# Hybrid SSD and linear-attention layer: output gates projected in the gate stages, scan steps at half pieces, first block from columns

## The chip, the cores and the metric

The kernel runs on one core of a Trainium2 chip, as one program. The metric is the device time of the whole program in microseconds (us). Engines are named as in the profile: PE (TensorE, the matrix engine), DVE (VectorE), ACT (ScalarE), POOL (GpSimd), SP (SyncE, which here issues most DMAs).

## The reference

One decoder layer over 16 meta tokens and 2048 real tokens of width 1024, in float32:

```
u = rmsnorm(h, norm_w);  proj = u @ w_in  -> z, xbc, dt, q, k, v, g_gla, a_lr, merge_g
xbc = silu(conv4(xbc))                       # Mamba-2 SSD branch, 16 heads in 4 groups
y_ssd = rmsnorm((ssd_scan(xbc, dt) + d_skip * xs) * silu(z)) * ssd_norm_w
log_a = log_sigmoid(a_lr @ gate_w2 + b) / 16 # gated linear attention (GLA), 4 heads
o = gla_scan(q / sqrt(128), k, v, log_a)     # S_t = diag(a_t) S_{t-1} + k_t^T v_t; o_t = q_t S_t
y_gla = rmsnorm(o) * gla_norm_w * silu(g_gla)
merged = sum over branches of sigmoid(merge_g) * (y_branch @ w_branch)
out = rmsnorm(h + merged @ w_out)[16:] * final_norm_w
```

`g_gla`, 1024 columns of `w_in` (256 a head), is the GLA branch's output gate. It is used only in `silu(g_gla)`.

## The kernel before

All float32 products are made of three matmuls in a split form: each operand is written as a high and a low part (`split`, `load_w`), and `accum` issues high x high, high x low and low x high (L186, L187, L188).

The **first part** walks through four blocks of 512 tokens (the first with the 16 meta tokens beside them). A block has eight pieces: four SSD groups (`ssd_proj`, pieces 0 to 3), then four GLA heads (`gla_proj`, pieces 4 to 7). A piece is a generator that issues projections of the normalised input `u` (PSUM tiles `pj`) and yields between them; at each yield `step()` advances by one step everything in the list `running`: the scan of the piece before (`ssd_scan`, `gla_scan`), the making of the gates, the fetching of the next block's `u` (`fetch_u`, which runs `load_u`), and sums for the second part (`beside_unit`). PE and SP work through their instructions in exactly the order in which this code issues them (`manual_schedule`); the order of the other engines is laid out by the scheduler.

A projected tile of 128 features (`proj_feat`) is 24 matmuls of 512 columns, in two halves of 12, each with its weights of 512 KB (`whl`), loaded by SP from a split copy in memory (`k_s`, `k_g`, `k_v`, `k_z`). In block 0 the weights come raw (`wr`), are split by ACT and POOL (L173, L174), and are stored for the other blocks. An SSD group has four features (numbers 0 to 15 over the groups, `k_s0` to `k_s15`); each goes through a convolution, of which ACT does the first steps (L466, L467) into a tile `acc`. A GLA head has q, k (one feature each), v (`proj_tok`, four quarters of 24 matmuls of 256 columns) and the two gate features (`gs`, L622 to L627): PE projects, ACT takes tanh (L625), and DVE makes (tanh + 1) times the gate (L626), so that `gla_scan` can multiply its result by it at its end (L796).

`gla_scan` begins when its head's projections are all issued, and so runs beside the next head's. It advances through levels of 64 down to 2 (`level_in`, `level_out`), then sums over features (L754), transposes (L769), and goes over four chunks: products into `pc`, one with the state `s_gla` (L780), then the state's update on DVE (L781), which reads `pc` and which the next chunk's L780 needs.

`load_u` for a block after the first reads the rows of x in four steps, each in two halves (L255 loads into a tile `acc`, L256 squares with a running sum on ACT), then the columns in eight steps (loaded into `acc`, scaled on DVE at L289, rounded to the high part by ACT at L291, stored, and the low part made on DVE at L293). `acc` has two buffers; the SSD convolution uses the same two.

The **second part** is seven stages (for each half of the tokens a gate stage and two branch stages; then the output), each a large product in the seven-product form: units of pairs of 2 x 2 blocks with the products in the order `PS`, 12 matmuls of 512 columns each (PSUM tiles `psa`, `psb`, `psc`), `use` for every finished quarter, `fetch` for what `use` needs, and sums of operands (`make_sums`) prepared beforehand. The gate stage makes tanh of `merge_g` in 8 such pairs. `at(position, action)` places loads and sums by position in the list of products.

Of the kernel before, what the change touches and what calls it, by code (L numbers as in the profile page):

```python
# [36 lines left out]
T_GATE = 32  # L37


@with_exitstack  # L40
def trunk_kernel(ctx: ExitStack, tc: tile.TileContext, xm, xmt, w_feat, w_tok, w_zm, w_br, w_o,
# [22 lines left out]
    y_left = [[[left(f"y{n}_{b}_{kt}") for kt in range(KT)] for b in range(nblk)] for n in range(2)]  # L64

# [35 lines left out]
    def braw_y(n, s):  # L101
        return lambda k, t: y_left[n][2 * s + t][k]
# [10 lines left out]
    for s in range(nsb):  # L113
        b = 2 * s + 2
        if b < nblk:
            beside.update({(b, 0): ("b", 0, s), (b, 4): ("b", 1, s)})
        else:
            late += [("b", 0, s), ("b", 1, s)]
        if 0 < s:
            beside[b - 1, 0] = ("g", s)  # L120
# [43 lines left out]
    def load_w(key, src):  # L164
        n = src.shape[-1]
        hl = mk(wpool, [P, 2, 512], F32R, "whl", bufs=4)[:, :, :n]
        if key in kept:
            nc.sync.dma_start(hl.bitcast(F32), kept[key])
        else:
            save(2)  # L170
            raw = mk(wpool, [P, 512], F32, "wr", bufs=NWR)[:, :n]
            nc.sync.dma_start(raw, src)
            nc.scalar.activation(hl[:, 0], raw, AF.Copy)  # L173
            nc.gpsimd.tensor_tensor(hl[:, 1], raw, hl[:, 0].bitcast(F32), op=ALU.subtract)  # L174
            kept[key] = wdram.tile([P, 2, n], F32, tag="k_" + key, name="k_" + key, bufs=1)
            unsaved.append((kept[key], hl.bitcast(F32)))
# [13 lines left out]
    def proj_feat(key, src, segs, moving):  # L190

        pss = [bank(pj, "pj") for _ in segs]
        for half in range(2):
            h, lo = load_w(f"{key}_{half}", src[:, half * 512:(half + 1) * 512])
# [7 lines left out]
    def proj_tok(key, src, u, starts, banks, width=256, per=2, sub=None):  # L202
# [5 lines left out]
        for q0 in range(0, nq, 2):  # L208
            if q0 == nq // 2:
                yield  # L210
            ws = [load_w(f"{key}_{q}", src[:, q * per * width:(q + 1) * per * width]) for q in (q0, q0 + 1)]
            for i, ((bk, ps), a) in enumerate(zip(banks, starts)):
                c0 = sub if sub is not None and i >= NCH else 0
# [23 lines left out]

    def load_u(b):
        m0 = META if b == 0 else 0
        row0 = META - m0 + b * BLK  # L240
        tt = m0 + BLK
        pair = mk(upool, [P, 2, KT * (META + BLK)], F32R, "u")[:, :, :KT * tt]
        uh, ul = [pair[:, i].rearrange("p (k t) -> p k t", k=KT) for i in range(2)]

        def rows_rstd(r0, n):
            ss = mk(sm, [P, 1], F32, "ss")
            if m0:
                xt = mk(wk, [P, D], F32, "tok4", bufs=NT4)
                nc.sync.dma_start(xt[:n], xm[r0:r0 + n, :])
                nc.scalar.activation(xt[:n], xt[:n], AF.Square, accum_out=ss[:n])  # L250
            else:
                s2 = mk(sm, [P, 2], F32, "ss2")
                for i in range(2):
                    xt = mk(wk, [P, META + BLK], F32, "acc")[:, :BLK]
                    nc.sync.dma_start(xt, xm[r0:r0 + n, i * BLK:(i + 1) * BLK])  # L255
                    nc.scalar.activation(xt, xt, AF.Square, accum_out=s2[:, i:i + 1])  # L256
                nc.vector.tensor_tensor(ss, s2[:, 0:1], s2[:, 1:2], op=ALU.add)
# [6 lines left out]
        for c in range(NCH):  # L264
            rs.append(rows_rstd(META + b * BLK + c * P, P))
            yield
        if m0:
            rs.append(rows_rstd(0, META))
            nc.sync.dma_start(cst[:, :2], cf32[:, :2])
            nc.sync.dma_start(pv, pvec)  # L270
# [3 lines left out]
        rbs = [(rb, m0, BLK)]  # L274
        if m0:
            rm = bank(pt, "pt")
            nc.tensor.matmul(rm[:, :META], rs[NCH][:META].to_broadcast([META, P]), ident[:META, :META],
                             start=True, stop=True)
            rbs = [(rm, 0, META)] + rbs
        else:  # L280
            rbc = mk(wk, [P, 3 + META + BLK], F32, "cin")[:, :BLK]
            nc.scalar.activation(rbc, rb, AF.Copy)
            rbs = [(rbc, 0, BLK)]
            yield
        for kt in range(KT):
            xk = mk(wk, [P, META + BLK], F32, "acc")[:, :tt]
            nc.sync.dma_start(xk, xmt[:, kt, row0:row0 + tt])
            for ps, a, n in rbs:
                nc.vector.scalar_tensor_tensor(xk[:, a:a + n], xk[:, a:a + n], norm_w[:, kt:kt + 1], ps[:, :n],  # L289
                                               op0=ALU.mult, op1=ALU.mult)  # L290
            nc.scalar.activation(uh[:, kt, :tt], xk, AF.Copy)  # L291
            nc.scalar.dma_start(u_left[b][kt], xk[:, m0:])
            nc.vector.tensor_tensor(ul[:, kt, :tt], xk, uh[:, kt, :tt].bitcast(F32), op=ALU.subtract)  # L293
# [8 lines left out]
    for _ in fetch_u(0):  # L302
        pass

# [17 lines left out]
    w2r = mk(wk, [P, META + BLK], F32, "act", bufs=NACT)[:48, :512]  # L322
# [119 lines left out]
    def ssd_proj(o, g):  # L442
# [16 lines left out]
        for j in range(4):  # L459
            ti = g * 4 + j  # L460
            pss = proj_feat(f"s{ti}", w_feat[T_SSD + ti], o.segs_all, o.mov)
# [24 lines left out]
    def ssd_scan(o, g, feats, zs):  # L486
# [88 lines left out]
        if m0:  # L575
            meta_state()
        for c in range(1, NCH):
# [9 lines left out]
        for j in range(2):  # L587
# [3 lines left out]
            yo = mk(wk, [P, BLK], F32, "gg", bufs=4)  # L591
# [4 lines left out]
    def gla_proj(o, h):  # L596
# [7 lines left out]
        for ps, (a, n) in zip(proj_feat(f"g{t0 + 1}", w_feat[t0 + 1], o.segs_all, o.mov), o.segs_all):  # L604
            nc.scalar.activation(kf[:, a:a + n], ps[:, :n], AF.Copy)
        yield
# [8 lines left out]
        yield from proj_tok(f"v{h}", w_tok[SG + h], o.u, o.starts + [0] * o.ci0, places)  # L615
# [4 lines left out]
        yield  # L620
        gs = []
        for j in range(2):  # L622
            ps, = proj_feat(f"g{t0 + 2 + j}", w_feat[t0 + 2 + j], o.segs_real, o.mov)
            gg = mk(wk, [P, BLK], F32, "gg", bufs=4)
            nc.scalar.activation(gg, ps, AF.Tanh, scale=0.5)  # L625
            nc.vector.scalar_tensor_tensor(gg, gg, 1.0, ps, op0=ALU.add, op1=ALU.mult)  # L626
            gs.append(gg)  # L627
            yield
        begin(gla_scan(o, h, qs, kf, (vh, vl), vm, gs))

    def gla_scan(o, h, qs, kf, vt, vm, gs):
# [160 lines left out]
        for j in range(2):  # L792
# [3 lines left out]
            nc.vector.scalar_tensor_tensor(gs[j], ps, hgw[:, j:j + 1], gs[j], op0=ALU.mult, op1=ALU.mult)  # L796
        yield
        for j in range(2):
            nc.scalar.dma_start(y_left[1][o.b][2 * h + j], gs[j])
# [4 lines left out]
    def begin(gen):  # L804
        begun.append(gen)

    def step():
# [12 lines left out]
    with tc.manual_schedule(engines={mybir.EngineType.PE, mybir.EngineType.SP}):  # L820
        for b in range(nblk):
            o = new_block(b, next_u[b])
            for i in range(SG + GH):
# [4 lines left out]
                if i == SG and b + 1 < nblk:  # L828
                    begin(fetch_u(b + 1))
                for _ in ssd_proj(o, i) if i < SG else gla_proj(o, i - SG):  # L830
                    step()
# [116 lines left out]
    def gate_stage(s):  # L948
        def use(n, i, t, ps, snap):
# [5 lines left out]
        return Stage(f"gate{s}", ("g", s), 8,  # L955
                     lambda n, i, j: w_feat[T_GATE + 2 * n + i, :, j * BLK:(j + 1) * BLK].rearrange(
                         "p (k c) -> p k c", c=P), use)
# [202 lines left out]
```

## Time and profile before

| | |
|---|---|
| median of 3 runs | 2352.43 us (2346.6 to 2354.13) |
| profiled execution | 2356.86 us, its span 2355.0 us |
| PE busy | 2255.4 us (96%) |
| DVE, ACT, POOL busy | 1562.0 (66%), 1189.1 (50%), 684.2 us (29%) |
| mean granted clock of PE | 0.98 |
| DMA | 518.06 MB, mean 220 GB/s |

Busy time is the union of an engine's instructions, so that PE at 96% of the span has about 100 us without any matmul. The chain that ended last is the work followed back from the last instruction, and a wait is named by the instruction whose end released it.

### The profile page before, as it was taken

The numbers are of one execution on the slowest core, as the hardware profiler recorded it, in microseconds if no ns is written. First come the engines' busy times: TensorE is split into PE (matmuls) and PEld (weight loads), VectorE is DVE, ScalarE is ACT, GpSimd is POOL, SyncE is SP. The second block draws the span as 40 slices with busy tenths as digits, with TensorE's granted clock in tenths as the row PEclk, the third lists the DMA queues.
The fourth block names the chain that finished last, engine by engine and source line by source line (L and its number), as shares of the span: only waits on it lengthen the run. The fifth ranks groups of instructions, "written<-read, shape, count | busy, mean of one in ns | idle before, by whom it ended". The sixth has DMA issues, their size and how long they took to land.

```text
span 2355.0 us, 36504 instructions
## 1 busy us (share of the span) xinstructions
PE 2255.4 (96%) x12641; PEld 1968.2 (84%) x12641; DVE 1562.0 (66%) x2889; ACT 1189.1 (50%) x2764; POOL 684.2 (29%) x681
## 2 busy tenths in 40 slices
PE   6899999999999999999999999889999999999998
PEld 6889889888888988888988898768788788777886
DVE  4676665676675667566558555664679854788876
ACT  4665655465544455543455443454554454544543
POOL 3343433122321212221122200207424254322441
PEclk8999999999999999999999999989999999999999
DMA  8665875666786666787666655456668866778752
GB/s 274 212 215 183 296 255 192 202 220 218 248 282 191 207 224 208 254 268 221 193 217 216 206 167 163 136 181 226 218 222 275 277 215 213 253 244 274 236 192 108
DMA packets 301546, 518.06 MB, mean 220 GB/s; under 512 B 27696, under 2 KB 143664, under 8 KB 301360
## 3 DMA queue, kind: packets, MB, share of 16 engines
q1 hardware_dynamic: 200112, 402.32, 52.7%
q10 hardware_dynamic: 101248, 113.41, 13.8%
q8 instruction: 99, 1.62, 0.3%
q14 instruction: 87, 0.71, 0.1%
HBM read 368.42 MB, written 147.19 MB: 219 GB/s over the span
## 4 chain that ended last, share of the span: by engine, by line
PE 66%; DMA 12%; DVE 10%; ACT 5%; issue 4%; POOL 2%; SPq 1%; ACTq 0%; DVEq 0%; POOLq 0%
PE pj L186 11%; PE pj L188 11%; PE pj L187 11%; PE psa L186 4%; PE psa L187 4%; PE psa L188 4%; PE psb L187 2%; PE psb L188 2%; PE psb L186 2%; DMA acc<-in_xmt 2%; PE pc L556 2%; DMA br<-br_t 2%; PE pc L690 1%; DVE b L894 1%; PE pc L780 1%
## 5 line engine op out<-in xcount | busy, mean ns | idle before, releaser
L186 PE MATMUL pj<-u,whl 128*128 128x512 f32 (+1 forms) x1184 | 447.4, 378 | 8.3 <-ACT g_all L429 3.3
L188 PE MATMUL pj<-u,whl 128*128 128x512 f32 (+1 forms) x1184 | 431.6, 365 | 0.8 <-POOL whl L174 0.8
L187 PE MATMUL pj<-u,whl 128*128 128x512 f32 (+1 forms) x1184 | 430.7, 364 | 0.0
L186 PE MATMUL pj<-whl,u 128*128 128x256 f32 (+1 forms) x992 | 291.5, 294 | 8.1 <-ACT u L291 5.5
L188 PE MATMUL pj<-whl,u 128*128 128x256 f32 (+1 forms) x992 | 285.2, 287 | 0.7 <-DVE u L293 0.7
L187 PE MATMUL pj<-whl,u 128*128 128x256 f32 (+1 forms) x992 | 285.1, 287 | 0.6 <-POOL whl L174 0.5
L186 PE MATMUL psa<-b,a 128*128 128x512 f32 x640 | 253.5, 396 | 19.0 <-ACT sn L934 17.0
L186 PEld LDWEIGHTS pj<-u,whl 128*128 128x128 f32 x1184 | 225.7, 191 | 46.2 <-ACT g_all L429 3.7
L188 PEld LDWEIGHTS pj<-u,whl 128*128 128x128 f32 x1184 | 225.2, 190 | 36.8 <-POOL whl L174 1.1
L187 PEld LDWEIGHTS pj<-u,whl 128*128 128x128 f32 x1184 | 225.7, 191 | 33.3
L187 PE MATMUL psa<-b,a 128*128 128x512 f32 x640 | 252.8, 395 | 0.0
L188 PE MATMUL psa<-b,a 128*128 128x512 f32 x640 | 252.5, 395 | 0.0
L918 DVE TENSOR_TENSOR a<-ar,a 128x512 fp32r<-128x512 f32 x160 | 151.1, 950 | 82.1 <-ACT a L917 81.9
L186 PEld LDWEIGHTS pj<-whl,u 128*128 128x128 f32 x992 | 192.3, 194 | 9.2 <-ACT u L291 6.0
L187 PEld LDWEIGHTS pj<-whl,u 128*128 128x128 f32 x992 | 192.4, 194 | 1.7 <-POOL whl L174 1.3
L188 PEld LDWEIGHTS pj<-whl,u 128*128 128x128 f32 x992 | 192.4, 194 | 1.5 <-DVE u L293 1.5
L80 POOL TENSOR_TENSOR wr<-wr 128x256 f32<-128x256 f32 x80 | 67.0, 838 | 432.0 <-DMA wr<-y 172.1
L174 POOL TENSOR_TENSOR whl<-wr,whl 128x512 fp32r<-128x512 f32 (+1 forms) x100 | 133.5, 1342 | 188.9 <-ACT whl L173 141.3
L908 POOL TENSOR_TENSOR as<-ar,ar 128x512 f32<-128x512 f32 x40 | 59.3, 1482 | 422.4 <-DMA ar<-in_w_feat 124.3
L894 DVE TENSOR_TENSOR b<-br,b 128x512 fp32r<-128x512 f32 x196 | 149.2, 784 | 45.3 <-ACT b L893 44.8
L471 DVE SCALAR_TENSOR_TENSOR acc<-cin,hcw,acc 128x512 f32<-128x512 f32 (+1 forms) x192 | 156.6, 816 | 24.7 <-ACT acc L467 24.1
L893 ACT ACTIVATE b<-br 128x512 fp32r<-128x512 f32 x196 | 119.1, 626 | 93.5 <-DMA br<-br_t 34.7
(267 smaller groups left out, 5077.9 us busy)
## 6 DMA issues: line engine op xcount, KB each, us to landing
whl<-k_s SPq DMA_DIRECT2D x96, 512.0 KB, 4.4
whl<-k_g SPq DMA_DIRECT2D x96, 512.0 KB, 4.1
whl<-k_v SPq DMA_DIRECT2D x48, 512.0 KB, 3.8
whl<-k_z SPq DMA_DIRECT2D x36, 512.0 KB, 3.8
wr<-in_w_feat SPq DMA_DIRECT2D x64, 256.0 KB, 4.5
k_s<-whl SPq DMA_DIRECT2D x32, 512.0 KB, 3.6
cb<-cumd ACTq DMA_DIRECT2D x64, 256.0 KB, 5.6
y<-gg ACTq DMA_DIRECT2D x64, 256.0 KB, 4.5
```

The source lines that it names most:

```text
L80: nc.gpsimd.tensor_tensor(o, x, y, op=ALU.subtract)
L174: nc.gpsimd.tensor_tensor(hl[:, 1], raw, hl[:, 0].bitcast(F32), op=ALU.subtract)
L186: nc.tensor.matmul(ps, sh, mh, start=first, stop=False, **kw)
L187: nc.tensor.matmul(ps, sh, ml, start=False, stop=False, **kw)
L188: nc.tensor.matmul(ps, sl, mh, start=False, stop=last, **kw)
L471: nc.vector.scalar_tensor_tensor(acc, cin[:, k:k + tt], hcw[:, ti, k:k + 1], acc, op0=ALU.mult, op1=ALU.add)
L556: nc.tensor.matmul(py[:, h * 64:(h + 1) * 64], dm[:, h], xdt[:, h], start=True, stop=True)
L690: nc.tensor.matmul(ps[:, r * P:(r + 1) * P], kq[:, 2 * r * P:(2 * r + 1) * P], kq[:, (2 * r + 1) * P:(2 * r + 2) * P], start=True, stop=True)
L893: nc.scalar.activation(t[:, 0], raw, AF.Copy)
L894: nc.vector.tensor_tensor(t[:, 1], raw, t[:, 0].bitcast(F32), op=ALU.subtract)
L908: nc.gpsimd.tensor_tensor(s1, a21, a22, op=ALU.add)
L918: nc.vector.tensor_tensor(t[:, 1], src, t[:, 0].bitcast(F32), op=ALU.subtract)
```

## The change

1. **The output gates move.** `gla_proj` no longer projects the gate features, and `gla_scan` no longer multiplies by them: its last step scales on ACT (`yo`) and stores. Each gate stage has four more pairs (12 in place of 8), the first eight alternating between the GLA heads' gates and merge gates. For a head's pair, `fetch` reads the stored `y`, and `use` multiplies it by the projected gate and by (tanh + 1) and stores the result (`yg_left`), which branch 1 then reads.
2. **Half steps.** `gla_proj` yields after every half piece with `HALF`; `step` counts fractions and advances a generator when its count reaches one. `gla_scan` is begun before the last half of its head, with a rate of 1.5. SSD groups still step by whole pieces.
3. **The next block's input** is begun with SSD group 3 (`i == SG - 1`), where it was begun with GLA head 0.
4. **The first block** takes its mean squares from the columns alone (`first_u`): eight column loads on two queues, squares on ACT, sums on DVE, and a product with ones; the stores of this `u` go to SP between the weight loads.
5. All sums of the GLA branch's results (`("b", 1, s)`) become late ones with new positions.

Core of the diff:

```diff
@@ gla_proj
-        ps, = proj_feat(f"g{t0}", w_feat[t0], o.segs_real, o.mov)
+        ps, = yield from proj_feat(f"g{t0}", w_feat[t0], o.segs_real, o.mov, HALF)
         nc.scalar.activation(qs[:, :BLK], ps, AF.Copy, scale=QSCALE)
-        yield
+        yield HALF
...
-        yield
-        gs = []
-        for j in range(2):
-            ps, = proj_feat(f"g{t0 + 2 + j}", w_feat[t0 + 2 + j], o.segs_real, o.mov)
-            gg = mk(wk, [P, BLK], F32, "gg", bufs=4)
-            nc.scalar.activation(gg, ps, AF.Tanh, scale=0.5)
-            nc.vector.scalar_tensor_tensor(gg, gg, 1.0, ps, op0=ALU.add, op1=ALU.mult)
-            gs.append(gg)
-            yield
-        begin(gla_scan(o, h, qs, kf, (vh, vl), vm, gs))
+        begin(gla_scan(o, h, qs, kf, (vh, vl), vm), 1.5)
+        yield HALF
@@ gla_scan, last steps
-            nc.vector.scalar_tensor_tensor(gs[j], ps, hgw[:, j:j + 1], gs[j], op0=ALU.mult, op1=ALU.mult)
-        yield
-        for j in range(2):
-            nc.scalar.dma_start(y_left[1][o.b][2 * h + j], gs[j])
+            yo = mk(wk, [P, BLK], F32, "gg", bufs=3)
+            nc.scalar.activation(yo, ps, AF.Identity, scale=hgw[:, j:j + 1])
+            nc.scalar.dma_start(y_left[1][o.b][2 * h + j], yo)
@@ step
-        for gen in list(running):
-            if next(gen, running) is running:
-                running.remove(gen)
+        for e in list(running):
+            e[2] = e[2] + part * e[1] if part else 1.0
+            if e[2] >= 1:
+                e[2] -= 1
+                if next(e[0], running) is running:
+                    running.remove(e)
@@ walk over blocks and pieces
-                if i == SG and b + 1 < nblk:
+                if i == SG - 1 and b + 1 < nblk:
                     begin(fetch_u(b + 1))
@@ first_u
+        for kt in range(KT):
+            xs.append(mk(wk, [P, META + BLK], F32, "act", bufs=NACT))
+            (nc.scalar if kt % 2 else nc.sync).dma_start(xs[kt], xmt[:, kt, :tt])
...
+        for kt in range(KT):
+            nc.scalar.activation(sq[kt // 2][:, kt % 2], xs[kt], AF.Square)
+            if kt:
+                nc.vector.tensor_tensor(total, total, sq[kt // 2][:, kt % 2], op=ALU.add)
@@ gate_stage, use
+            if head(n) is not None:
+                y = got.pop((n, i, t))
+                nc.vector.tensor_tensor(y, y, x, op=ALU.mult)
             th = io() if snap is None else snap
             nc.scalar.activation(th, x, AF.Tanh, scale=0.5)
-            store(g_left[2 * s + t][2 * n + i], th)
+            if head(n) is not None:
+                nc.vector.scalar_tensor_tensor(y, th, 1.0, y, op0=ALU.add, op1=ALU.mult)
+                store(yg_left[2 * s + t][2 * head(n) + i], y)
+            else:
+                store(g_left[2 * s + t][2 * gate(n) + i], th)
```

How this moves instructions is seen in the order of single engines. First SP in block 1, before: the weight loads of SSD features 13 to 15 and, after the dots, of the second GLA feature of head 0 (`k_g17`); `whl` is a weight tile, `acc ... <-in_xm` one half of the next block's rows.

```order
L168 DMA whl_1143_7060<-k_s13_0_2570 128x1024
L168 DMA whl_1144_7074<-k_s13_1_2601 128x1024
L76 DMA wr_1148_7100<-in_w_o 128x256 x2
L76 DMA wr_1149_7101<-in_w_o 128x256 x2
L168 DMA whl_1161_7144<-k_s14_0_2685 128x1024
L168 DMA whl_1162_7158<-k_s14_1_2716 128x1024
L168 DMA whl_1176_7224<-k_s15_0_2798 128x1024
L168 DMA whl_1177_7238<-k_s15_1_2829 128x1024
...
L255 DMA acc_1196_7332<-in_xm 128x512
L255 DMA acc_1197_7335<-in_xm 128x512
L168 DMA whl_1201_7344<-k_g17_0_2957 128x1024
L168 DMA whl_1202_7358<-k_g17_1_2988 128x1024
```

The rows were read among the GLA features, two loads ahead of `k_g17`. Now the same queue in the same block, from feature 12 on:

```order
L171 DMA whl_1090_6697<-k_s12_0_2481 128x1024
L171 DMA whl_1091_6711<-k_s12_1_2512 128x1024
L309 DMA acc_1107_6778<-in_xm 128x512
L309 DMA acc_1108_6781<-in_xm 128x512
L171 DMA whl_1111_6789<-k_s13_0_2590 128x1024
L171 DMA whl_1112_6803<-k_s13_1_2621 128x1024
L78 DMA wr_1116_6829<-in_w_o 128x256 x2
L78 DMA wr_1117_6830<-in_w_o 128x256 x2
L309 DMA acc_1130_6874<-in_xm 128x512
L309 DMA acc_1131_6877<-in_xm 128x512
L171 DMA whl_1134_6885<-k_s14_0_2717 128x1024
L171 DMA whl_1135_6899<-k_s14_1_2748 128x1024
```

A pair of row loads now stands ahead of the weights of feature 13, and another ahead of those of feature 14.

ACT before, around the squares of those rows (`pj_1160` and `pj_1175` are the products of features 14 and 15):

```order
L466 ACTIVATE cin_1163_7172<-pj_1160_7143 128x512
L467 ACTIVATE acc_1164_7173<-pj_1160_7143,hcb_359,hcw_357 128x512
...
L466 ACTIVATE cin_1178_7252<-pj_1175_7223 128x512
L467 ACTIVATE acc_1179_7253<-pj_1175_7223,hcb_359,hcw_357 128x512
L256 ACTIVATE acc_1196_7332,ss2_1195_7331<-acc_1196_7332 128x512
L256 ACTIVATE acc_1197_7335,ss2_1195_7331<-acc_1197_7335 128x512
```

And now (`pj_1089` is the product of feature 12, `acc_1107` and `acc_1108` are the two halves of the rows):

```order
L501 ACTIVATE cin_1092_6725<-pj_1089_6696 128x512
L502 ACTIVATE acc_1093_6726<-pj_1089_6696,hcb_371,hcw_369 128x512
L581 ACTIVATE sq_1143_6940<-sq_1143_6940 128x512
L519 DMA cb_1196_7237<-cumd_772_4918 128x4x128
L576 ACTIVATE bt_1099_6750<-pt_1096_6741 128x128
L310 ACTIVATE acc_1107_6778,ss2_1106_6777<-acc_1107_6778 128x512
L310 ACTIVATE acc_1108_6781,ss2_1106_6777<-acc_1108_6781 128x512
L606 ACTIVATE junk_1104_6774,ssq_1077_6663<-tok4_1076_6662 128x256
L509 ACTIVATE act_1094_6734<-acc_1093_6726 128x512
```

The squares of a pair of row halves stood behind the convolution of feature 15, the last of the group; now they stand behind that of feature 12, and those of the next pair (not shown) behind that of feature 13.

PE in `gla_scan` of a head in block 1, before: from a sum over features (`pt_1434`) to the product with the state. The dots ahead of the second transposing pair and ahead of `pc` each stand for the rest of 24 matmuls of one gate feature, those behind the first `pc` for its other five.

```order
L754 MATMUL pt_1434_8661<-sq_1426_8612,ones_r_245 128x512
L186 MATMUL pj_1438_8672<-u_420_2935,whl_1439_8673 128x512
...
L769 MATMUL pt_1442_8706<-cst_243,sq_1435_8665 128x128 x2
L186 MATMUL pj_1444_8712<-u_420_2935,whl_1445_8713 128x512
...
L186 MATMUL pc_1451_8750<-tok4_1318_7945,kdt_1392_8395 128x256
...
L780 MATMUL pc_1451_8750<-s_gla_250,act_1379_8319 128x256
```

And now, in a head of the same block; here the dots stand for the rest of 24 matmuls of a part of v:

```order
L783 MATMUL pt_1362_8115<-sq_1352_8044,ones_r_277 128x512
L191 MATMUL pj_1356_8050<-whl_1366_8126,u_312_2338 128x256
...
L798 MATMUL pt_1368_8154<-cst_275,sq_1363_8119 128x128 x2
L191 MATMUL pj_1357_8051<-whl_1366_8126,u_312_2338 128x256
...
L191 MATMUL pc_1371_8191<-tok4_1275_7622,kdt_1320_7906 128x256
...
L809 MATMUL pc_1371_8191<-s_gla_282,act_1307_7832 128x256
```

The steps of the scan stood 24 matmuls of 512 columns apart, and now stand 24 of 256 columns apart.

More of the change, by code (lines that the diff above doesn't have):

```diff
@@ L300, in fetch_u @@
         next_u[b] = yield from load_u(b)
[L302 to L303 removed]
+    next_u[0] = first_u()
     nc.sync.dma_start(cst[:, 2:], cf32[:, 2:])
@@ L614, in gla_proj @@
             places.append((2, pv5[:, :256]))
-        yield from proj_tok(f"v{h}", w_tok[SG + h], o.u, o.starts + [0] * o.ci0, places)
+        yield from proj_tok(f"v{h}", w_tok[SG + h], o.u, o.starts + [0] * o.ci0, places, part=HALF)
         if m0:
```

167 lines of the change are left out of this document (104 added, 63 removed).

## The prediction

> **What bounds the kernel now.** I read the page first, then the waits of PE by stretch, then the timelines of the two places that the change moves.
>
> ```profile
> span 2355.0 us, 36504 instructions
> PE 2255.4 (96%) x12641; PEld 1968.2 (84%) x12641; DVE 1562.0 (66%) x2889; ACT 1189.1 (50%) x2764; POOL 684.2 (29%) x681
> PE 66%; DMA 12%; DVE 10%; ACT 5%; issue 4%; POOL 2%; SPq 1%; ACTq 0%; DVEq 0%; POOLq 0%
> ```
>
> PE is busy for 96% of the span, and no other engine for more than 66% (DVE). So a matmul taken away is time gained, as long as everything that PE needs still comes in time; the chain's 12% on DMA and 10% on DVE say where it might not. The waits of PE in block 1 from its last SSD group on, then those of the stretch from 765 to 1475 us, and last those of the second part, with the total, the count and the longest in us:
>
> ```profile
> PE pc L780 <- DVE s_gla L781: 3.0, 1, 3.0
> PE pc L556 <- DVE sq L547: 1.7, 1, 1.7
> PE pj L186 <- DMA whl<-k_g: 0.9, 1, 0.9
> ...
> PE pc L780 <- DVE s_gla L781: 4.8, 3, 2.5
> PE pc L556 <- DVE sq L547: 1.8, 1, 1.8
> PE pj L186 <- DMA whl<-k_g: 0.6, 1, 0.6
> ...
> PE psa L186 <- ACT sn L934: 17.0, 6, 4.3
> ```
>
> In blocks 1 to 3 PE loses very little: the rows that the trace lists are ten waits in 900 us, the longest 3.0 us. The order of work has been fitted so that weights, rows and scan steps arrive just in time, and the change takes cover from two of these fits.
>
> **Matmuls that go.** Consecutive starts on PE give the price of one matmul; the last two rows are from the table of windows (length, then busy time of PE, PEld, DVE, ACT, POOL, the granted clock, DMA share, GB/s):
>
> ```profile
> 693.75 0.39 PE L186 MATMUL pj<-u,whl 128*128 128x512 f32 x1
> 693.97 0.39 PE L187 MATMUL pj<-u,whl 128*128 128x512 f32 x1
> ...
> 707.65 0.28 PE L187 MATMUL pc<-tok,kdt 128*128 128x256 f32 x1
> 707.77 0.28 PE L188 MATMUL pc<-tok,kdt 128*128 128x256 f32 x1
> ...
> 707.00:765.00 58.00, 55.00 (x323) 48.59 (x322) 33.44 (x76) 23.71 (x70) 8.07 (x9) 0.97 0.60 191
> ...
> 1590.00:1649.00 59.00, 59.00 (x262) 48.87 (x261) 28.57 (x32) 26.07 (x46) 43.65 (x41) 1.00 0.68 224
> ```
>
> A 512-wide one takes 0.22 to 0.23 us (262 of them fill the 59.00 us of the last row: 0.225), a 256-wide one 0.12. The change removes the two gate projections of each GLA head from the first part: 16 heads x 2 x 24 = 768 matmuls. It adds four pairs to each of the two gate stages, at seven products of 12 matmuls: 2 x 4 x 84 = 672. All are 512 wide, all on a full PE: 96 x 0.227 = 21.8 us less. By the Trainium skill (page "TensorE: Matmul & The Clock Gate", section "Back-to-back issue gap") a warm 512-wide matmul follows the last after 512/2.4 + 2.5 = 216 ns, which would make it 20.7; the trace here shows a little more, and I keep the trace's. The gate's ACT and DVE work moves with it; the gate stage has room for it, with DVE busy 28.57 and ACT 26.07 of 59 us.
>
> **The row loads go into the last SSD group.** This is the largest term. The next block's rows are now read during SSD group 3 and no longer during GLA head 0. What such a load does to the queue behind it can be seen at its present place. Rows of SP (issuing), ACT and PE of block 1:
>
> ```profile
> 588.49 9.63 SPq L168 DMA_DIRECT2D whl<-k_s  x4
> 611.22 5.82 SPq L255 DMA_DIRECT2D acc<-in_xm  x2
> 617.15 0.85 SPq L168 DMA_DIRECT2D whl<-k_g  x2
> ...
> 592.24 0.63 ACT L546 ACTIVATE sq<-sq 128x512 f32<-128x512 f32 x1 [2.61 <-POOL wr L80]
> 606.89 0.28 ACT L541 ACTIVATE bt<-pt 128x128 f32<-128x128 f32 x1 [0.22 <-DVE tok L538]
> 614.81 0.60 ACT L466 ACTIVATE cin<-pj 128x512 f32<-128x512 f32 x1 [1.04 <-PE pc L559]
> 615.30 0.78 ACT L467 ACTIVATE acc<-pj,hcb,hcw 128x512 f32<-128x512 f32 x1
> 615.96 0.63 ACT L256 ACTIVATE acc<-acc 128x512 f32<-128x512 f32 x1
> ...
> 612.75 1.00 PE L556 MATMUL pc<-c,sq 128*128 128x64 f32 x8
> 614.07 0.59 PE L559 MATMUL pc<-c,bt 128*128 128x256 f32 x2
> 621.01 0.50 PE L186 MATMUL pj<-u,whl 128*128 128x512 f32 x1 [0.86 <-DMA whl<-k_g]
> ```
>
> The two halves of a row load go through `acc`, which has two buffers and is also the SSD convolution's. The second half waits on SP until ACT has squared the first (L256), that square stands in ACT's order behind the convolution's start (L466, L467), and the weight loads stand behind both on SP. So from L466 (614.81) it is 2.3 us to the issue of the `k_g` loads (617.15) and 6.2 us to the matmul that needs them (621.01). It costs 0.86 us only because, between that feature's matmuls and the waiting ones, PE has a scan step (612.75 to about 614.5) and another feature, q, of 24 x 0.227 = 5.4 us, whose weights were already there.
>
> In the new place the same chain stands between one SSD feature and the next, twice in a group: the loads for features 13 and 14 are issued behind a row's second half, and that waits for ACT behind L501 and L502 of the feature just before. The cover is then the scan step alone, 2.1 us. The chain: 0.2 us from the last matmul to ACT, the 6.2 us above, and the two ACT rows that now stand in between (0.63 and 0.28, shortened by their overlap to 0.8) make 7.2; less 2.1 of cover it is 5.1 us, four times in blocks 1 and 2: +20.4. Before, the four `k_s` loads of 588.49 were issued a piece ahead and cost PE nothing. The ends: 3 us each where ACT takes the square early, 6.5 where the loads land slower. For the second there is a reason, since DMA is full in that group already (1.03 below), and 2 MB of rows come into it.
>
> ```profile
> 589.00:597.00 8.00, 8.00 (x43) 6.79 (x42) 5.60 (x12) 4.38 (x11) 4.57 (x6) 1.00 1.03 323
> ...
> whl<-k_s SPq DMA_DIRECT2D x96, 512.0 KB, 4.4
> wr<-in_w_feat SPq DMA_DIRECT2D x64, 256.0 KB, 4.5
> ...
> L174 POOL TENSOR_TENSOR whl<-wr,whl 128x512 fp32r<-128x512 f32 (+1 forms) x100 | 133.5, 1342 | 188.9 <-ACT whl L173 141.3
> ```
>
> A weight load of 512 KB takes 4.4 us to land. By the Trainium skill (page "DMA: Bandwidth & Descriptors", section "Anatomy of one DMA — SWDGE (gpsimd) path": about 2.0 us and then bytes at 436 GB/s) it would be 3.2 us, an estimate for a single transfer on another issue path, and each stall would be 1.2 us shorter. With some 200 to 320 GB/s already moving the row is what counts.
>
> In block 0 the features' weights come raw (4.5 us) and go through a split on ACT and POOL (1.3 us for POOL's part), with the store of the last ones queued between. That is longer by 1 to 2 us than in the other blocks, but the split of the loads into halves lets part of it run ahead: 3 to 8 us each; I take 5, twice: +10. The column loads that now precede the k weights cost 0 to 4 us in each of three blocks: +6, less the waits that go with the old place, 0.9 and 0.6 above and about 2.5 in block 0: +2. While PE stands still, ACT and DVE catch up, and the two waits on L547 (1.7 and 1.8) go: -3.5.
>
> **Steps at half pieces.** Between the scan's products of the last level (L754, now L783) and its state update (L781, now L810) PE used to do 48 matmuls of 512. Now it does 48 of 256, the v pieces: 48 x (0.227 - 0.12) = 5.1 us less cover. How near the limit this was, in block 1:
>
> ```profile
> 695.79 0.63 PE L754 MATMUL pt<-sq,ones_r 128*128 128x512 f32 x2
> 712.50 1.22 PE L780 MATMUL pc<-s_gla,act 128*128 128x256 f32 x2 [2.96 <-DVE s_gla L781]
> ...
> 698.69 0.68 DVE L626 SCALAR_TENSOR_TENSOR gg<-gg,pj 128x512 f32<-128x512 f32 x1
> 699.28 0.44 DVE L756 COPY_PREDICATED c<-msk,pt 128x256 f32<-128x256 uint8 x1
> 704.92 1.22 DVE L289 SCALAR_TENSOR_TENSOR acc<-acc,pv,cin 128x512 f32<-128x512 f32 x1
> 708.34 0.68 DVE L293 TENSOR_TENSOR u<-acc,u 128x512 fp32r<-128x512 f32 x1
> 711.97 0.47 DVE L781 SCALAR_TENSOR_TENSOR s_gla<-s_gla,egl,pc 128x256 f32<-128x256 f32 x1
> ```
>
> PE came from the last L754 (ends about 696.2) to the L780 that needs the update after 13.3 us, at 709.5, and then stood 2.96 us. It now comes after 13.3 - 5.1 = 8.2. DVE took 12.7 us from L756 to L781 here, with 1.8 us of next-block work (L289, L293) and one L626 of 0.6 in it. In the new order the gate's row is gone, but two rows of v's split (about 0.6 each) come in, and two of the scan's levels now stand behind the update: at the spacing of these rows, 0.6 us for 512 columns and 0.34 for 256, the sixteen rows from L785 to L810 take 7.7 us. With 0.7 from product to DVE and 0.5 for the update it is 8.9 to 9.0, against 8.2: some 0.8 us a head, and 2.5 in the heads in which next-block rows fall between. The second v piece ends only 1.7 us (14 x 0.12) ahead of the waiting matmul, and its split, two rows and the update need about 3.0: 1.3. I take 1.3 for 14 heads (the last has no cover of this kind, and one of block 0 is held elsewhere): 18, less the waits on L781 that are there now (3.0 + 4.8): +10. Ends: 0 and +25.
>
> **The clock.** The stall of 2.96 us is in a window with a granted clock of 0.97 over 58 us: 0.03 x 58 = 1.7 us lost behind it. Each of the six stalls of about 5 us should cost the same: +10, with 0 and +20 as ends. The rule of the Trainium skill ("TensorE: Matmul & The Clock Gate", "What's actually happening") has the clock halved after an idle window of about 3.4 us and whole again after about 3.4 busy; that also gives 1.7 each, but nothing for a stall as short as 2.96, which did cost it in this trace.
>
> **The rest.** The first block is now built from columns alone:
>
> ```profile
> 15.74 0.61 PE L186 MATMUL pj<-whl,u 128*128 128x288 f32 x1 [2.58 <-ACT whl L173]
> 47.10 0.38 ACT L456 ACTIVATE tok<-pt 128x256 f32<-128x256 f32 x1 [0.83 <-PE pt L188]
> ```
>
> The first projection starts at 15.74 and its last result is read at 47.10. Eight squares in a row on ACT and eight sums on DVE put the start some 6 to 11 us later, but all of u is then there, and the projection waits for weights alone; so it ends about where it did: 0, between -4 and +6. The late sums and the y loads go into stretches of the second part where PE already waits 17.0 us at six transitions: +2, between -2 and +6. The final scaling that goes from DVE to ACT is hidden by PE.
>
> The sum: -21.8 + 20.4 + 10 + 2 - 3.5 + 10 + 10 + 2 = +29. The profiled execution took 2356.86 us (its span is 2355.0), 4.4 above the median of 2352.43; 2356.9 becomes 2386, and the median 2381.
>
> **The rivals.**
> *The covers hold* (faster). The squares run early and the weights of features 13 and 14 arrive while ACT is ahead, DVE keeps up with the shorter steps, and only the matmuls count: -21.8 and +2: 2333. For it speaks that DVE and ACT have idle time (66% and 50%); against it that the second half of a row can't start before ACT's square, and the square stands behind the feature just done. It decides if the stall per feature is under 1 us. Chance 0.19.
> *They cancel.* Stalls of 3 us in place of 5 (+12 and +6), some 0.6 us a head in the scans (no more than the waits that go) and half the loss of clock (+5): -21.8 + 18 + 2 - 3.5 + 5 + 2 = +2, 2354, within 0.3% (2345 to 2359) of before, which is about what a measurement of this kernel can tell from no change. It is the sum with each unknown cost near its lower end. Chance 0.1.
> *A full DMA makes it worse.* With the rows in a group that reaches a share of 1.03, loads land after 6 to 7 us and not 4.4, block 0 loses 8 per feature, and each head stalls for 2.2: +29 + 12 + 6 + 12 = 59, about 2411. Against it: the stretch after 597 is back at a share of 0.69. Chance 0.12.
> The forecast keeps 0.59.
>
> **How the numbers follow.** Faster by over 0.3%: the first rival and a rest of the forecast's lower end, 0.2. Same: 0.1. Slower: 0.7. The forecast's own bounds are 2360 to 2402. The range is stretched to most of both outer rivals: 2333 to 2406.
>
> **What would show it.** In the profile after: PE waiting some 5 us for `whl<-k_s` twice in each SSD group 3 of blocks 0 to 2, and none of it in block 3, which fetches no rows; the SP rows of those loads right behind `acc<-in_xm`; 768 matmuls fewer in the first part and 672 more in the second; waits of L809 on L810 of 1 to 2 us in most heads; the granted clock under 1 in these places. Wrong if `whl<-k_s` doesn't appear among PE's waits: then the first rival is right. Also wrong in size if the second part is longer by more than 672 x 0.227 = 153 us plus 2, or the first block's projection ends far from 47 us.

## The result and the profile after

The changed kernel takes 2436.95 us (median of 4 runs, 2435.72 to 2441.56) against 2353.28 of before (4 runs): a ratio of 1.0349, 95% interval 1.0329 to 1.0369. The direction was forecast; the amount, some 84 us, lies outside the range, which ended at 2406.

The head of the page of the changed kernel, with the lines that answer to those of before:

```profile
span 2435.0 us, 36543 instructions
PE 2260.0 (93%) x12555; PEld 1967.8 (81%) x12555; DVE 1631.1 (67%) x2964; ACT 1243.9 (51%) x2860; POOL 731.2 (30%) x693
PE 56%; DMA 16%; DVE 11%; ACT 7%; issue 5%; POOL 3%; SPq 2%; ACTq 1%; POOLq 0%; DVEq 0%
```

PE has lost 3 points of its busy share, and DMA's part of the chain has grown from 12% to 16%. The waits of PE over the whole span of the changed kernel (total, count, longest in us), cut to the lines that matter here:

```profile
PE pj L191 <- DMA whl<-k_s: 21.4, 4, 5.7
...
PE pj L191 <- ACT whl L178: 18.1, 3, 9.2
PE pc L809 <- DVE s_gla L810: 13.3, 12, 2.8
...
PE pj L191 <- ACT acc L502: 11.3, 6, 4.2
PE pj L191 <- DMA whl<-k_g: 8.0, 2, 5.2
PE pc L719 <- DVE c L602: 7.5, 5, 2.9
PE pc L719 <- DVE s_ssd L597: 7.5, 6, 2.6
PE pc L591 <- DVE sq L582: 5.3, 3, 2.5
```

The first line, the four waits for `k_s`, did not exist before. The same view of the kernel before, for the lines that correspond (L467 to L502, L547 to L582, L690 to L719, L781 to L810):

```profile
PE pc L780 <- DVE s_gla L781: 9.2, 6, 3.0
...
PE pj L186 <- ACT whl L173: 5.1, 2, 2.6
...
PE pc L556 <- DVE sq L547: 3.5, 2, 1.8
...
PE pj L186 <- DMA whl<-k_g: 1.5, 2, 0.9
...
PE pc L690 <- DVE s_gla L718: 1.1, 1, 1.1
PE pj L186 <- ACT acc L467: 1.1, 3, 0.5
PE pc L690 <- DVE c L697: 1.0, 1, 1.0
PE pc L690 <- ACT junk L785: 0.9, 1, 0.9
```

To see where the time lies, each trace is divided at three kinds of marks: the first convolution row of a block on ACT (L466, now L501), its first q row (L601, now L637), and the first `psa` matmul of the second part. "SSD" is from the first mark to the second, "heads" from the second to the next block, summed over four blocks, in us of the profiled executions.

| kernel | start | SSD of blocks 0, 1, 2, 3 | SSD sum | heads sum | second part | span |
|---|---|---|---|---|---|---|
| before | 53.2 | 184.2, 165.7, 165.3, 167.7 | 682.9 | 818.5 | 800.5 | 2355.0 |
| changed | 50.2 | 214.2, 187.6, 186.1, 167.9 | 755.9 | 672.5 | 956.4 | 2435.0 |
| e1 | 50.5 | 185.0, 172.0, 168.2, 165.8 | 691.1 | 673.3 | 955.4 | 2370.3 |
| e5 | 50.0 | 190.5, 171.7, 174.4, 165.8 | 702.4 | 663.5 | 954.9 | 2370.8 |
| e7 | 49.9 | 181.0, 165.4, 165.8, 165.5 | 677.6 | 665.4 | 954.9 | 2347.8 |

The heads should have lost 768 x 0.227 = 174.3 us and the second part should have gained 672 x 0.227 = 152.5. So against the matmul count the changed kernel's start is 3 us shorter, its SSD parts are 73 longer, its heads 28 longer and its second part 3.4 longer. With -21.8 for the matmuls that is +80, the difference of the spans. Block 3, which fetches nothing, has the old SSD length. The runs e1, e5 and e7 in the table are explained below; e7's profiled execution (2349.85 us) is one of its fastest, 9 us under its median.

### The profile page after: what moved, and what is told of

The parts are those of the page before. It is cut to its first block, busy times and chain, and to the rows that moved or that the text cites. A ratio compares the mean times of both kernels' runs of the same rounds, so it can differ in the third digit from the quotient of the medians.

```text
span 2435.0 us, 36543 instructions
## 1 busy us (share of the span) xinstructions
PE 2260.0 (93%) x12555; PEld 1967.8 (81%) x12555; DVE 1631.1 (67%) x2964; ACT 1243.9 (51%) x2860; POOL 731.2 (30%) x693
## 4 chain that ended last, share of the span: by engine, by line
PE 56%; DMA 16%; DVE 11%; ACT 7%; issue 5%; POOL 3%; SPq 2%; ACTq 1%; POOLq 0%; DVEq 0%
PE pj L191 8%; PE pj L193 8%; PE pj L192 8%; PE psa L191 5%; PE psa L192 4%; PE psa L193 4%; PE psb L192 2%; PE psb L193 2%; PE psb L191 2%; PE pc L719 1%; ACT sq L579 1%; DVE a L949 1%; DMA wr<-in_w_tok 1%; DMA io<-yg 1%; PE pc L809 1%
## 5 line engine op out<-in xcount | busy, mean ns | idle before, releaser
L191 PE MATMUL pj<-u,whl 128*128 128x512 f32 (+1 forms) x928 | 355.3, 383 | 63.6 <-DMA whl<-k_s 21.4
L193 PE MATMUL pj<-u,whl 128*128 128x512 f32 (+1 forms) x928 | 340.4, 367 | 1.5 <-POOL whl L179 1.4
L192 PE MATMUL pj<-u,whl 128*128 128x512 f32 (+1 forms) x928 | 339.1, 365 | 0.0
L191 PE MATMUL psa<-b,a 128*128 128x512 f32 x768 | 304.6, 397 | 20.5 <-ACT sn L965 18.1
L193 PE MATMUL psa<-b,a 128*128 128x512 f32 x768 | 303.3, 395 | 0.0
L192 PE MATMUL psa<-b,a 128*128 128x512 f32 x768 | 303.1, 395 | 0.0
L191 PEld LDWEIGHTS pj<-u,whl 128*128 128x128 f32 x928 | 184.6, 199 | 96.1 <-DMA whl<-k_s 23.0
L949 DVE TENSOR_TENSOR a<-ar,a 128x512 fp32r<-128x512 f32 x192 | 189.5, 993 | 84.2 <-ACT a L948 81.9
L193 PEld LDWEIGHTS pj<-u,whl 128*128 128x128 f32 x928 | 183.1, 197 | 29.6 <-POOL whl L179 3.4
L192 PEld LDWEIGHTS pj<-u,whl 128*128 128x128 f32 x928 | 184.9, 199 | 23.7
L939 POOL TENSOR_TENSOR as<-ar,ar 128x512 f32<-128x512 f32 x48 | 71.8, 1496 | 431.3 <-DMA ar<-in_w_feat 162.1
L191 PEld LDWEIGHTS psa<-b,a 128*128 128x128 f32 x768 | 146.8, 191 | 55.1 <-ACT sn L965 22.1
L192 PEld LDWEIGHTS psa<-b,a 128*128 128x128 f32 x768 | 146.9, 191 | 31.0 <-DVE b L925 0.4
L193 PEld LDWEIGHTS psa<-b,a 128*128 128x128 f32 x768 | 146.5, 191 | 30.8
```

Of the source, the lines that this page charges most:

```text
L191: nc.tensor.matmul(ps, sh, mh, start=first, stop=False, **kw)
L192: nc.tensor.matmul(ps, sh, ml, start=False, stop=False, **kw)
L193: nc.tensor.matmul(ps, sl, mh, start=False, stop=last, **kw)
L939: nc.gpsimd.tensor_tensor(s1, a21, a22, op=ALU.add)
L949: nc.vector.tensor_tensor(t[:, 1], src, t[:, 0].bitcast(F32), op=ALU.subtract)
```

## The experiments

**The place of the fetch.** e1 is the changed kernel, and e3 the kernel before, with the one line turned round.

```diff
e1:  -                if i == SG - 1 and b + 1 < nblk:
     +                if i == SG and b + 1 < nblk:
e3:  the reverse, in the kernel before
```

> The changed kernel with one line undone: the next block's input is begun with GLA head 0 again, not with SSD group 3. Theory A (the place of the fetch: row halves in the convolution's two buffers, squared behind the convolution, with the weight loads queued behind them) expects the SSD parts of blocks 0 to 2 back at their old lengths, 30 + 22 + 21 = 73 us less, and a few us given back in the heads, where the twelve steps of the fetch now have shorter pieces to hide behind: about 2370 us. Theory B (the half steps starve PE all over, the fetch being only where it shows) expects less than 25 us, 2412 or more.

> The kernel before with one line of the change alone: the next block's input begun with SSD group 3. Theory A expects the same waits for k_s as in the changed kernel, and the SSD parts of blocks 0 to 2 longer by about 73 us, less up to 10 us that the fetch no longer costs in the heads: 2415 to 2425. If the early fetch only hurts together with the half steps, it stays within 20 us of 2353.

e1 took 2370.76 us (ratio to before 1.0058, 1.0038 to 1.0077), 66 less than the changed kernel. e3 took 2420.92 (1.0274, 1.0245 to 1.0304): this line alone makes the old kernel 64 us slower. Its waits on weights:

```profile
PE pj L186 <- ACT whl L173: 24.5, 6, 7.5
PE pj L186 <- DMA whl<-k_s: 21.7, 4, 6.0
PE pj L186 <- DMA whl<-k_g: 10.8, 2, 5.6
```

They are of the same kind as in the changed kernel, `k_s` to within 0.3 us, without moved gates or half steps. In e1 no wait for `k_s` is left. Theory A holds; theory B, that half steps starve PE all over, falls as the main cause.

**What in the place hurts.** Timelines of the changed kernel, block 1, the stretch between features 13 and 14: SP, ACT, PE.

```profile
593.89 9.54 SPq L309 DMA_DIRECT2D acc<-in_xm  x2
603.53 1.80 SPq L171 DMA_DIRECT2D whl<-k_s  x4
...
600.68 0.60 ACT L501 ACTIVATE cin<-pj 128x512 f32<-128x512 f32 x1 [7.45 <-PE pj L193]
601.18 0.77 ACT L502 ACTIVATE acc<-pj,hcb,hcw 128x512 f32<-128x512 f32 x1
602.36 0.62 ACT L310 ACTIVATE acc<-acc 128x512 f32<-128x512 f32 x1
...
592.75 0.80 PE L191 MATMUL pj<-u,whl 128*128 128x512 f32 x1 [5.67 <-DMA whl<-k_s]
608.00 0.79 PE L191 MATMUL pj<-u,whl 128*128 128x512 f32 x1 [5.26 <-DMA whl<-k_s]
```

The first half of a row was there early: its load was issued at 593.89. But ACT squares it only at 602.36, behind L501 and L502, for which it waited 7.45 us; SP sits on the second half until then, and issues the weights of feature 14 at 603.53. PE had nothing to do from 602.7 to 608.0. That is the chain of the prediction, step by step: from L501 to the waiting matmul it takes 7.3 us, where 7.0 was forecast. Two explanations remained: the shared buffer, or the 2 MB of rows in a full DMA. e5 gives the rows two buffers of their own and changes nothing in the order of SP. Its second edit makes room for them: with the first alone (e2) the buffers do not fit the on-chip memory, by 0.2 KB a partition, and there is no time.

```diff
-                xt = mk(wk, [P, META + BLK], F32, "acc")[:, :BLK]
+                xt = mk(wk, [P, BLK], F32, "xr", bufs=2)
...
-            yo = mk(wk, [P, BLK], F32, "gg", bufs=3)
+            yo = mk(wk, [P, BLK], F32, "gg", bufs=2)
```

> The changed kernel with the next block's rows loaded into two buffers of their own, not the convolution's two (room is made by two gg buffers in place of three); the fetch stays in SSD group 3 and SP's order as in the changed kernel. If the shared buffers make the stalls (theory A1), a second row half waits for nothing, the k_s waits of 5 to 6 us go in blocks 1 and 2 and the two of 7 to 9 us in block 0: 45 to 60 us less, 2377 to 2392. If it is the 2 MB of rows in a group whose DMA is full (theory A2), the waits stay at 4 us or more and the time is within 15 us of 2437.

e5 took 2377.26 us (1.0093, 1.0064 to 1.0121). Its waits on weights are now:

```profile
PE pj L191 <- DMA whl<-k_g: 9.5, 2, 6.6
PE pj L191 <- ACT whl L178: 2.3, 1, 2.3
```

With the same loads in the same order, all waits for `k_s` and nearly all for the raw weights of block 0 are gone: it was the buffers (A1). What stays is `k_g`, where the columns still go through `acc`. The same in the changed kernel: SP in block 1, what SP waited for between 621.95 and 632 us, and PE:

```profile
629.27 0.33 SPq L329 DMA_DIRECT2D acc<-in_xmt  x1
...
631.60 0.38 SPq L171 DMA_DIRECT2D whl<-k_g  x1
...
SPq L329 <- DMA u<-acc: 6.9, 1, 6.9
...
636.29 0.79 PE L191 MATMUL pj<-u,whl 128*128 128x512 f32 x1 [5.25 <-DMA whl<-k_g]
```

SP holds the second column load for 7 us. It waits for the first column, whose buffer is free only when its store (`u<-acc`) has landed; the other buffer of `acc` is with a convolution. The next `k_g` load is issued behind it, at 631.60. That columns with buffers of their own would end this wait is not tested.

**The first block.** e4 is the kernel before with `first_u` alone (the fourth point of the change).

```diff
-    for _ in fetch_u(0):
-        pass
+    next_u[0] = first_u()
```

> The kernel before with the new first block alone (columns only, the sums by PE, the stores of u on SP). The traces put the end of the first projection 3 us earlier: 2350. If the later part of block 0 pays for the stores on SP (the waits on L502 in block 0 that only the changed kernel has), it is 2355 to 2360 instead.

2354.61 us (1.0000, 0.9979 to 1.0021): nothing that can be measured. The 3 us at the start are there in the trace (its first convolution row comes at 50.6) and are given back in block 0, whose SSD part is 188.2 in place of 184.2. The change also has one step more in the SSD scans of block 0 (a `yield` behind `meta_state()`), which is not among the five points above and which no run has alone.

**Half steps and the heads.** e1 still has heads that are 29 us longer than the matmul count says. In e6 and e7 only the starting fraction of a scan is changed, on top of e1, so that its steps fall on other half pieces. In e8, also on top of e1, there are no half steps, and a scan takes four steps a head in place of six.

```diff
-        begun.append([gen, rate, 1 - rate * HALF if rate > 1 else 0.0])
e6:  +        begun.append([gen, rate, 0.5 if rate > 1 else 0.0])
e7:  +        begun.append([gen, rate, 0.0 if rate > 1 else 0.0])
e8:  -HALF = 0.5
     +HALF = None
     -        begin(gla_scan(o, h, qs, kf, (vh, vl), vm), 1.5)
     +        begin(gla_scan(o, h, qs, kf, (vh, vl), vm))
```

> The fetch begun with GLA head 0 (as in e1_fetch_at_head0), and the scans' fraction begun at 0.5 in place of 0.25: every scan step falls on another half piece, so that between the last sum and the transposes PE now has 48 matmuls of 256 in place of 24, and from the sum to the state's product 72 in place of 48, 2.9 us more, while two early levels lie closer. If the cover in this place sets the waits of L809 on L810 (theory C), those fall from 18 us to under 8 and the time by 8 to 14 us with the clock behind them: 2357 to 2363. If DVE's work per head is the limit (theory D), the waits only move to other lines: within 4 us of 2371.

> As e6_phase_half with the fraction begun at 0: here the wider cover lies between the transposes and the state's product (24 of 256, then 24 of 256 and 12 of 512), and half the cover ahead of the last two chunks goes. Theory C: the L809 waits of the first chunks fall as in e6, but some come back at the later chunks: 2360 to 2368. Theory D: within 4 us of 2371.

> The fetch begun with GLA head 0, the gates moved as in the changed kernel, but no half steps: a head has four steps of whole pieces, so that a scan runs over two and a half heads, each step behind 24 matmuls of 512 or 48 of 256. Theory C (the short cover of half steps costs some 25 us in the heads) expects the L809 waits gone and 2345 to 2360, if the buffers of three scans at once suffice. If instead the loss comes from the steps that several scans now take at once, on DVE, it is 2371 or more.

e6: 2368.85 us (1.0061, 1.0044 to 1.0078), the same as e1. e7: 2358.65 (1.0006, 0.9987 to 1.0026), 12 less than e1 and level with before. e8: 2429.26 (1.0313, 1.0293 to 1.0334), 58 more. So the half steps are no loss by themselves; without them, with four steps a head, the moved gates cost far more. A part of that is of another kind: e8 has 16.5 us of waits for ACT to read the tile `pt` (its rows L628 and L826), where e1 has 3.9. Theory D named e6 rightly (within 4 us of 2371); for e7 both theories miss, and theory C was wrong in its detail. The waits in e1, then in e7:

```profile
PE pc L809 <- DVE s_gla L810: 18.0, 13, 2.7
PE pc L719 <- DVE c L602: 7.9, 6, 2.6
...
PE pc L719 <- DVE s_ssd L597: 2.9, 6, 1.4
...
PE pc L809 <- DVE s_gla L810: 15.9, 10, 4.5
PE pc L719 <- DVE s_ssd L597: 2.4, 3, 1.4
PE pc L719 <- DVE c L602: 2.3, 2, 1.2
```

The waits on the state's update hardly moved, though the cover ahead of them was larger by half. What went are the waits of L719, the small matmuls of the levels, on DVE's work for the SSD scan that still runs (L597, L602); in e1 all L719 rows add up to 20.4 us, in e7 to 7.5. They do not explain all of it. The two profiled executions differ by 22.5 us (the medians by 12), and by the table only 7.9 of these lie in the heads; 13.5 lie in the SSD parts, 4.0 of them in block 0, ahead of any GLA scan. So a part of what these two traces show is not the phase's doing.

**How many steps a head.** e9 is e7 with the rows' own buffers; e10 also has the early fetch; e11 and e12 are e9 with other rates.

```diff
e11: -        begin(gla_scan(o, h, qs, kf, (vh, vl), vm), 1.5)
     +        begin(gla_scan(o, h, qs, kf, (vh, vl), vm), 1.25)
e12: +        begin(gla_scan(o, h, qs, kf, (vh, vl), vm), 1.75)
```

> Phase zero (e7) with the rows in two buffers of their own (two gg buffers); the fetch begins with GLA head 0. The last k_g wait of 1.0 us and the waits of head 0 that follow from the fetch should shrink: 2352 to 2358, not told apart from before. If the waits there come from the SSD scan's tail on DVE and not from the row loads, it stays at e7's 2359.

> As e9, but the fetch begins with SSD group 3 as in the changed kernel. e5 against e1 put the early fetch with own buffers 6 us behind the late one: about 2363 here. If the early place is good in itself (its columns fall in head 0 earlier and leave heads 1 and 2 free), it is under e9: 2350 or less.

> As e9, with the scans at 1.25 steps a whole piece in place of 1.5: five steps a head, each behind more matmuls, but every scan longer, so that two and at times three are open at once. If cover per step is what counts: 2345 to 2352. If it is how many scan steps meet in one place (as in e8, with four steps a head and 58 us more than e1): 2365 or more.

> As e9, with the scans at 1.75: seven steps a head, shorter scans, less cover for each step. If cover per step is what counts: 2365 to 2380. If overlap of scans is what counts: 2350 or less.

e9: 2356.56 us (0.9995, 0.9980 to 1.0010), no difference to before and too close to e7 to say what the buffers bring here. e10: 2362.93 (1.0021, 1.0004 to 1.0038): the early place stays worse by some 6 us even without the shared buffers, as e5 was against e1, which is at the edge of the noise. e11: 2391.74 (1.0139), e12: 2386.66 (1.0118): it is worse on both sides, so that each theory has one of the two runs against it. The traces, divided as above, show two places. Against that of e9, which was its longest execution, that of e11 is 26.4 us longer, of which 21.3 lie in the SSD parts (711.8 against 690.5), into which its longer scans reach; that of e12 is 21.9 longer, of which 14.8 lie in the heads (679.6 against 664.8). So neither cover per step nor the overlap of scans decides alone.

**DVE in the heads.** e13 is e7 with level 16 of the scans left out, so that its scores are missing from the result: some 1.9 us less DVE work a head.

```diff
-        level_in(16)
...
-        level_out(16)
```

> Phase zero (e7) with level 16 of each GLA scan left out (its five DVE rows, two ACT rows and two small matmuls; the attention scores of that distance are then missing from the result). Those DVE rows, some 1.9 us, stand between the last sum of one head and its state update, since the next head's early levels come there. If DVE's queue in that place is what L809 waits for, its waits fall from 15.9 us to under 8 and the time by 10 to 20 us: 2338 to 2349. If the waits come from elsewhere (PE's own spacing, ACT), the time falls by no more than the 16 x 2 small matmuls, 3 us, to about 2355.

2340.44 us (0.9945, 0.9920 to 0.9971), 18 less than e7. The profiled executions differ by 10.1: the heads are 17.3 shorter (648.1 against 665.4), the SSD parts 4.5 and the second part 3.3 longer. In this kernel L807 is what L809 was:

```profile
PE pc L807 <- DVE s_gla L808: 11.3, 8, 2.8
```

About 1.1 us a head comes back for 1.9 us of DVE work taken out, and the small matmuls are at most 3 us of it. That fits a PE that waits for DVE in the heads. Two ACT rows a head went as well, though, so the run does not separate the two engines, and the update's wait does not carry it alone: it fell from 15.9 to 11.3, less than expected.

## Why the prediction was right and wrong

**Right: the sign, the largest mechanism, and the wait of one stall.** It named 5.1 us for each wait on `k_s`, four of them in blocks 1 and 2 (20.4): measured 21.4 in four. The rival "the covers hold" asked for a stall under 1 us and is refuted by that line; "a full DMA" is refuted by e5.

**Right: the matmuls.** The second part is 155.9 us longer, 152.5 by count and 3.4 beside (forecast +2; its sign of being wrong, more than 2 beside the count, is passed by about 1 us).

**Where the sum failed.** The span grew by 80 us where +29 was forecast. By the two pages PE is without a matmul for 175.0 us in place of 99.6, 75 more; the terms for waits came to +41. And its matmuls took some 26 us more than their count says (busy 2260.0 in place of 2255.4, where the count gives 21.8 less; an estimate, since the ends of matmuls are modelled); the term for the clock was +10.

**Wrong: the rest of the row and column chain, sized at +10, +2 and -3.5.** In block 0 the timeline of the changed kernel has, on SP and on PE:

```profile
213.12 14.88 SPq L309 DMA_DIRECT2D acc<-in_xm  x2
228.53 0.42 SPq L175 DMA_DIRECT2D wr<-in_w_feat  x1
230.15 0.49 SPq L175 DMA_DIRECT2D wr<-in_w_feat  x1
...
215.94 0.59 PE L191 MATMUL pj<-u,whl 128*128 128x264 f32 x1 [9.25 <-ACT whl L178]
233.86 0.59 PE L191 MATMUL pj<-u,whl 128*128 128x264 f32 x1 [6.56 <-ACT whl L178]
```

With 0.59 us for the low part (POOL, L179) behind each of the two, that is 17.0 us where I took 10, on the ground that the halves of a load run ahead. They don't: both raw loads stand behind the second row half. For the columns I took +6 for three blocks without looking for the buffers of `acc` in their chain, as I had done for the rows, and then took off waits of the old place: `k_g` alone is 8.0 in place of 1.5, and where a wait of 2.5 us on raw weights was to go from block 0, one of 2.3 is still there. And the waits on L547 (now L582) did not go (-3.5 forecast): 5.3 in place of 3.5.

**Wrong: the clock, sized at +10.** Windows (length, busy times of PE, PEld, DVE, ACT and POOL, then the granted clock, DMA share and GB/s). First the SSD parts of blocks 0 and 1 before, then the same two now; then the changed kernel behind its three stalls of over 5 us in block 1; last a stretch of the kernel before.

```profile
53.20:237.40 184.20, 171.17 (x1293) 163.33 (x1292) 127.20 (x230) 115.69 (x294) 71.67 (x73) 0.96 0.62 209
455.60:621.30 165.70, 164.62 (x972) 143.91 (x971) 113.73 (x237) 91.16 (x226) 37.76 (x60) 1.00 0.69 221
...
50.20:264.40 214.20, 181.37 (x1296) 171.94 (x1295) 126.52 (x234) 122.18 (x309) 74.29 (x75) 0.90 0.57 193
445.90:633.40 187.50, 168.78 (x969) 146.07 (x967) 114.95 (x238) 100.14 (x245) 38.45 (x62) 0.97 0.61 202
...
590.50:597.40 6.90, 4.65 (x11) 3.69 (x12) 2.05 (x6) 1.74 (x6) 1.42 (x3) 0.51 0.77 271
607.60:611.00 3.40, 3.00 (x7) 2.43 (x8) 0.40 (x1) 0.07 (x1) 0.16 (x1) 0.50 0.93 371
634.90:641.80 6.90, 5.51 (x13) 4.35 (x14) 1.44 (x2) 1.34 (x3) 2.18 (x3) 0.51 1.01 379
...
1210.80:1214.10 3.30, 3.30 (x18) 3.30 (x17) 0.68 (x1) 1.42 (x5) 0.00 (x0) 0.50 0.00 1
```

Block 0's SSD part has 19.8 us more without a matmul and 10.2 more of matmuls, which make its 30; block 1's has 17.6 and 4.2, which make its 22.

Behind the three stalls of block 1 PE worked 4.65, 3.00 and 5.51 us at half the clock. Half of that is lost: 2.3, 1.5 and 2.8 us, where I took 1.7 for each. (The third, for `k_g`, ends at 636.29 and counts to the heads.) Over all blocks the SSD parts have 19 us more of matmuls. The heads have 10 more than the count says, and for them the sum had no loss of clock at all. Shorter stalls can cost it too: in the kernel before, PE waited 1.87 us for L781 ahead of 1209.24, and the last line shows the half clock soon behind it. Not every such stall does: behind one of 1.82 us in the changed kernel, at 319.64, the granted clock was 1.00.

The rule of the Trainium skill (page "TensorE: Matmul & The Clock Gate", section "What's actually happening": half the clock after an idle window of about 3.4 us, full again after about 3.4 us of work) gives an estimate of 1.7 for each stall. Only the second stall, with 1.5, is near it; the half clock behind the first and the third lasted twice as long, and the wait of 1.87 us is shorter than that window.

**Half wrong: the heads, +10 against +28.** By the same kind of windows over all four blocks, 18 of the 28 are time without a matmul and 10 the slower matmuls. The waits on the update were sized at 1.3 us in 14 heads, +10 over those of before; there were 12 of 1.1 on average (13.3, +4.1), which is near. The `k_g` waits of 8.0 fall in the heads as well. Put at nothing, without a reason, was what the shorter heads do to all the other steps: L719 waits of 17.3 us (7.5 + 7.5, and three small rows of 2.3 together) where L690 had 3.0. I named one pair of steps with too little cover and left the others, though all of the scan's work in a head had lost 48 matmuls, 10.9 us, of cover. (The waits on L502, 11.3 where L467 had 1.1, are not in the heads: 8.1 of them are in block 0 up to 264 us. e1 has 12.0 of them and an SSD part of block 0 of 185.0, within 1 us of before, so they took the place of other waits.) That the lost cover is the cause fits e13, in which less DVE work gives time back, but it is argued and not shown: no run moves the gates and keeps the cover, and e8 shows only that the half steps are not the cost. What exactly each of e6, e7, e11 and e12 moves among the scan's steps stays open.

No version measured with the whole result beats the kernel before: e7 and e9 are level with it.

## What to carry to other kernels

When a load is moved to another place, follow its whole chain there: the buffer that it reuses, the instruction that frees that buffer, what stands ahead of that instruction on its engine, and every load that is queued behind it. Having found such a chain once, look for it at each transfer of the same group and in each variant of the stage, with the first pass (raw weights) as a case of its own; the wait that was named was sized well, and the ones beside it, with the slower clock behind them all, made up the difference. Matmuls that hide other engines' work may not be free to remove: here the heads gave 146 us where the count promised 174. What such matmuls covered is to be summed over all steps of the stage, not at the narrowest one.

## What was not expected of the hardware

A queue that is not held runs far ahead. SP in e5, block 1:

```profile
562.26 0.32 SPq L171 DMA_DIRECT2D whl<-k_s  x1
575.68 0.33 SPq L329 DMA_DIRECT2D acc<-in_xmt  x1
```

The rows and weights of group 3 were all issued by 562.26 us, then nothing for 13 us (the column load waits for its buffer), and there was no wait for `k_s`, though the bytes and their order were those of the changed kernel. So the DMA share of 1.03 that the prediction counted against this place was no limit; the time at which the loads could be issued was.
